# The gate product of a decoder block as seven products of halves, its last weight splits in vacated buffers, part of its gates added to x by transfers

## The chip, the cores and the metric

One Trainium2 chip, one of its cores. The metric is the device time of one execution in microseconds (us), the median of several runs. A profiled execution lists every instruction of the core's engines: TensorE (PE) with its weight loads (PEld), VectorE (DVE), ScalarE (ACT), GpSimd (POOL) and SyncE (SP), and the transfers that SP, ACT and POOL issue.

## What is computed

A decoder block on 512 rows of 1024 numbers, all in float32. Everything ahead of the last two products (a normalisation, one wide projection, a short convolution, four heads of a chunked recurrent attention, two output products) is cut here; it ends in `merged`. What matters:

```python
x = x + jnp.einsum('bsd,de->bse', merged, w_o[l])
gate = jax.nn.sigmoid(jnp.einsum('bsd,de->bse', rmsnorm(x, g_ple[l]), w_ple_gate[l]))
x = x + gate * jnp.einsum('bsp,pd->bsd', p[l], w_ple[l])
return rmsnorm(x, g_final)
```

Both weights are 1024 x 1024. The product with `w_ple` is made at the start of the kernel and waits in DRAM. `rmsnorm` is a row's factor times a column's: the column factor `g_ple` is multiplied in when x is turned, the row factor is the scale of the sigmoid.

## The kernel before

A float32 product is made of three TensorE passes on numbers cut in two: `hi` (rounded to float32r by ScalarE) and `lo` (the rest, a subtraction on VectorE). `mm3` (L215) issues hi*hi, hi*lo and lo*hi, each 128 rows x 128 x 512 columns. So every weight operand of 512 x 512 (1 MB, four blocks of 128 rows) is loaded by SP into one of four buffers (`load_raw`, L138), and split by halves of two blocks (`split_half`, L161): a ScalarE copy of 1024 elements a partition (L164), a VectorE subtraction of as many (L165). The split parts live in a ring of two operands (`wsplit`), so an operand can be split only when TensorE is done with the one two before it.

Most products are Strassen products in Winograd's form (`strassen`, L286): seven products of halves for eight, on sums of the operands. Sums on the weight side are made in the raw buffers, mostly by transfers that add (L171: POOL issues them after the split of a half, from the weight in DRAM); sums on the left side are made on VectorE. Sums of results are made by copying a bank of PSUM to SBUF (a snap, L333) and adding the next product's bank on VectorE (L337).

Work is written down in program order and each engine keeps that order. A generator (`tick`, `step`, L198 to L209) is stepped after every unit, the 12 matmuls of one row tile with one operand: first the newest tasks, then one half of a split from `pieces`, then the older tasks in `active`. A task's second piece is thus in the queues a unit later, and an instruction that waits holds back everything behind it on its engine.

The last two products are plain. `merged` is turned (the transposes `pth`, L1102) and cut into `mg`. The product with `w_o` has 16 units: two column halves, four row tiles, two operands. Each result tile goes through `add_residual` (L1163): a VectorE addition into `xr` (L1165), a ScalarE square with a row sum (L1167). `turn_to` (L1123) transposes x on TensorE (`ptk`, L1135) and cuts it into `h2` with `g_ple`. The gate's product has again 16 units. On its first column half `gated` (L1209) does a sigmoid from PSUM (ScalarE, L1213), a multiplication by the embedding `ple` (VectorE, L1214) and an addition into x (VectorE, L1215); then come the square (L1218) and x times `g_final` on POOL (L1224). `power` (L1242) takes a row's mean square to the power -1/2 on POOL (L1245), `final_scale` (L1247) refines it on VectorE, and `final` (L1254) makes the output tile and sends it out. On the last column half this follows tile by tile, the last tile in two column quarters of 256.

Of the kernel before, what the change touches and what calls it, by code (L numbers as in the profile page):

```python
# [14 lines left out]
P = 128  # L15
S = 512
# [20 lines left out]
def hybrid_block(ctx, tc, x, p, g_mix, w_in, conv_w, conv_b, w_a_out, b_gates, g_head,  # L37
# [117 lines left out]
    def split_tiles(i, h):  # L155

        parts = [wsplit.tile([P, HH, CW], F32R, name=f"w{u}{i}{h}", tag=f"w{u}{h}", align_bytes=256)
                 for u in ("hi", "lo")]
        splits.setdefault(i, []).append(parts)
        return raws[operands[i][0]][:, HH * h:HH * h + HH, :], *parts  # L160
# [19 lines left out]
    def queue_split():  # L180
        i = state["split"]
        if i < len(operands):
            state["split"] = i + 1
            pieces.extend((i, h) for h in range(2))
# [817 lines left out]
    m = mp.tile([P, NT, D], F32, name="m", tag="m")  # L1002
# [120 lines left out]
    def turn_to(dst, src, n, scale):  # L1123

        ks = range(n * HC, (n + 1) * HC)
        yield
        pts = {}
        for i in range(3):
            if i > 0:
                for k in ks[2 * i - 2:2 * i]:  # L1130
                    cut(dst[0][:, k, :], dst[1][:, k, :], pts[k], scale[:, k:k + 1])
            for k in ks[2 * i:2 * i + 2]:
                pts[k] = ps_x.tile([P, S], F32, name="ptk", tag="x")
                for t in range(NT):
                    pe.transpose(pts[k][:, t * P:(t + 1) * P], src[:, t, k * P:(k + 1) * P], ident)  # L1135
            yield


    ep_ctx, ep = open_pool("end")
    h2_ctx, h2p = open_pool("h2", side="right")  # L1140
    h2 = [h2p.tile([P, KT, S], F32R, name=f"h2_{i}", align_bytes=256) for i in range(2)]
    xr = ep.tile([P, NT, D], F32, name="xr")
    gfin = ep.tile([P, D], F32, name="gfin")
    ple = ep.tile([P, NT, D], F32, name="ple")
    ess = ep.tile([P, NT, 2], F32, name="ess")
    etot = ep.tile([P, NT], F32, name="etot")
    er = ep.tile([P, NT], F32, name="er")
    etmp = [ep.tile([P, NT], F32, name=f"etmp{i}") for i in range(3)]
    half = [slice(0, CW), slice(CW, D)]

    def load_end():
# [5 lines left out]
        for t in range(NT):  # L1157
            yield
            nc.gpsimd.dma_start(ple[:, t, :], ple_d[:, t, :])
        nc.gpsimd.dma_start(gfin, g_final.partition_broadcast(P))  # L1160

    def add_residual(n):
        def post(t, ps):  # L1163
# [4 lines left out]
            yield  # L1168
        return post

    ends = load_end()
    next(ends)
    active.append(ends)
    post = add_residual(0)
    pss = [None] * NT
    w = {}
    for c, ts in ((1, (0, 1)), (0, (0, 1)), (1, (2, 3)), (0, (2, 3))):
        if c not in w:  # L1180
            w[c] = next_operand(len(w) == 0)
        for t in ts:
            if c == 1:
                pss[t] = bank(t)
            for kt in range(HC):
                mm3(pss[t], [u[:, c * HC + kt, t * P:(t + 1) * P] for u in mg], [u[kt] for u in w[c]],
                    c == 1 and kt == 0, c == 0 and kt == HC - 1)
            if (c, t) == (1, 3):
                queue_split()
            step(post(t, pss[t]) if c == 0 else None)  # L1190
    active.append(turn_to(h2, xr, 0, gp))
    block_tm([(mg, 0), (mg, HC)], add_residual(1))
    active.append(turn_to(h2, xr, 1, gp))

    def norm_scale():
        yield
# [6 lines left out]
        dve.tensor_tensor(er, r, e, ALU.mult)  # L1203

    active.append(norm_scale())
    fss = ep.tile([P, NT, 4], F32, name="fss")
    xg = mp.tile([P, NT, D], F32, name="xg", tag="m")[:, :, half[0]]

    def gated(ps, t, c):  # L1209

        sl = xr[:, t, c]
        g = temp("e")[:, :c.stop - c.start]
        act.activation(g, ps, AF.Sigmoid, scale=er[:, t:t + 1])  # L1213
        dve.tensor_tensor(g, g, ple[:, t, c], ALU.mult)  # L1214
        dve.tensor_tensor(sl, sl, g, ALU.add)  # L1215

    def squares(t, c, i):
        act.activation(temp("c")[:, :c.stop - c.start], xr[:, t, c], AF.Square, accum_out=fss[:, t, i:i + 1])  # L1218

    def gate_embedding(t, ps):  # L1220
        gated(ps, t, half[0])
        yield
        squares(t, half[0], 0)
        pool.tensor_tensor(xg[:, t, :], xr[:, t, half[0]], gfin[:, half[0]], ALU.mult)  # L1224

    block_tm([(h2, 0), (h2, HC)], gate_embedding)

    base = ep.tile([P, NT], F32, name="base")
    wl = []

    def last_part(t, cs, a, b, ps):
        for c in cs:
            if c == len(wl):
                wl.append(next_operand())
            for kt in range(HC):
                mm3(ps[:, :b - a], [u[:, c * HC + kt, t * P:(t + 1) * P] for u in h2],
                    [u[kt][:, a:b] for u in wl[c]], c == 0 and kt == 0, c == 1 and kt == HC - 1)
            tick()
# [87 lines left out]
```

## Time and profile before

| what | value |
|---|---|
| median of 3 runs (lowest, highest) | 858.34 us (857.92, 858.58) |
| the profiled execution: its time, its span | 858.12 us, 856.3 us |
| mean granted TensorE clock | 0.997 |
| busy share: PE, DVE, ACT, POOL | 99%, 74%, 56%, 25% |
| first matmul of the product with w_o | 756.28 us |
| first matmul of the gate's product | 802.37 us |
| last matmul | 847.89 us |
| last output tile made | 852.5 us |

The span runs from the first to the last instruction of the core; the profiled execution's own time is 1.8 us more. Times inside the span are us from its start. A row of the timeline has a start, a duration, an engine, the line in the kernel, what is written and read, the shape, and in brackets how long the engine had been idle and for whom. The duration of a matmul is its passage through a pipeline; how far apart two starts lie is what it costs.

### The profile page before, as it was taken

What the parts mean: (1) busy time and instruction counts of PE and PEld (TensorE: products, weight loads), DVE (VectorE), ACT (ScalarE), POOL (GpSimd) and SP (SyncE); (2) the same over time, 40 slices, a digit from 0 to 9 for tenths busy, and PEclk for the clock granted to TensorE, in tenths of its full rate; (3) what the DMA queues carried; (4) which work ended last, traced back from release to release, by engine and by line L of the source; (5) the groups of instructions that cost most, each with busy time, mean ns of one, the idle gap of its engine ahead of it and who ended that gap; (6) DMA issues with size and microseconds to landing.
All of it is one profiled execution on the core that took longest, in us unless ns stands there. A gap on an engine that the chain in (4) does not pass through costs nothing.

```text
span 856.3 us, 12144 instructions
## 1 busy us (share of the span) xinstructions
PE 845.6 (99%) x4658; PEld 735.4 (86%) x4658; DVE 630.3 (74%) x813; ACT 483.4 (56%) x702; POOL 218.1 (25%) x221
## 2 busy tenths in 40 slices
PE   8999999999999999999999999999999999999996
PEld 6888888887889988888888999999998888888885
DVE  6786667976777676788677779897885788964465
ACT  6477665657755566665766654545543256634343
POOL 5103222203224332220223333342410222130031
PEclk9999999999999999999999999999999999999998
DMA  9749669779958998796998689999998487884002
GB/s 313 267 136 179 161 129 220 196 265 238 267 117 205 243 220 183 180 214 197 266 236 218 137 218 179 184 179 185 181 359 291 83 200 190 222 323 145 1 1 98
DMA packets 100139, 167.58 MB, mean 196 GB/s; under 512 B 5421, under 2 KB 45921, under 8 KB 98801
## 3 DMA queue, kind: packets, MB, share of 16 engines
q0 software_dynamic: 38672, 70.86, 43.0%
q1 hardware_dynamic: 58544, 90.97, 32.3%
q10 hardware_dynamic: 2864, 4.98, 1.6%
q8 instruction: 36, 0.59, 0.3%
q14 instruction: 23, 0.18, 0.1%
HBM read 150.01 MB, written 16.78 MB: 195 GB/s over the span
## 4 chain that ended last, share of the span: by engine, by line
PE 95%; DVE 2%; DMA 1%; issue 1%; ACT 1%; SPq 0%; POOL 0%; POOLq 0%; ACTq 0%
PE mm L217 29%; PE mm L218 29%; PE mm L219 29%; PE pv L217 1%; PE pv L219 1%; PE pv L218 1%; DMA xin<-in_x 1%; PE pty L799 1%; PE sc L219 1%; PE sc L218 1%; PE sc L217 1%; PE ptk L1135 0%; PE pth L1102 0%; PE pt L536 0%; DVE xin L531 0%
## 5 line engine op out<-in xcount | busy, mean ns | idle before, releaser
L165 DVE TENSOR_TENSOR wlo<-wraw,whi 128x1024 fp32r<-128x1024 f32 x238 | 298.3, 1256 | 118.6 <-ACT whi L164 117.8
L164 ACT ACTIVATE whi<-wraw 128x1024 fp32r<-128x1024 f32 x240 | 251.1, 1054 | 103.4 <-PE mm L219 44.5
L171 POOL DMA_DIRECT2D wraw<-in_w_in x112 | 136.7, 1418 | 316.9 <-DVE wlo L165 244.4
L333 ACT ACTIVATE s<-mm 128x512 f32<-128x512 f32 x84 | 50.2, 598 | 100.9 <-PE mm L219 99.6
L217 PE MATMUL mm<-whi,hs 128*128 128x512 f32 x256 | 99.9, 390 | 0.0
L218 PE MATMUL mm<-wlo,hs 128*128 128x512 f32 x256 | 99.8, 390 | 0.0
L219 PE MATMUL mm<-whi,hs 128*128 128x512 f32 x256 | 99.7, 389 | 0.0
L217 PE MATMUL mm<-hn_hi,whi 128*128 128x256 f32 (+1 forms) x304 | 93.4, 307 | 0.0
L219 PE MATMUL mm<-hn_hi,wlo 128*128 128x256 f32 (+1 forms) x304 | 93.0, 306 | 0.0
L218 PE MATMUL mm<-hn_lo,whi 128*128 128x256 f32 (+1 forms) x304 | 92.9, 306 | 0.0
L217 PE MATMUL mm<-hs,whi 128*128 128x256 f32 x320 | 90.9, 284 | 0.0
L218 PE MATMUL mm<-hs,whi 128*128 128x256 f32 x320 | 90.5, 283 | 0.0
L219 PE MATMUL mm<-hs,wlo 128*128 128x256 f32 x320 | 90.5, 283 | 0.0
L217 PE MATMUL mm<-whi,hn_hi 128*128 128x512 f32 x192 | 75.3, 392 | 0.0
L218 PE MATMUL mm<-wlo,hn_hi 128*128 128x512 f32 x192 | 75.0, 390 | 0.0
L219 PE MATMUL mm<-whi,hn_lo 128*128 128x512 f32 x192 | 74.7, 389 | 0.0
L218 PEld LDWEIGHTS mm<-hs,whi 128*128 128x128 f32 x320 | 61.4, 192 | 0.0
L217 PEld LDWEIGHTS mm<-hs,whi 128*128 128x128 f32 x320 | 61.4, 192 | 0.0
L219 PEld LDWEIGHTS mm<-hs,wlo 128*128 128x128 f32 x320 | 61.4, 192 | 0.0
L219 PEld LDWEIGHTS mm<-hn_hi,wlo 128*128 128x128 f32 x304 | 58.1, 191 | 2.8 <-POOL wlo L165 0.3
L218 PEld LDWEIGHTS mm<-hn_lo,whi 128*128 128x128 f32 x304 | 58.1, 191 | 2.4
L217 PEld LDWEIGHTS mm<-hn_hi,whi 128*128 128x128 f32 x304 | 58.1, 191 | 2.4
(306 smaller groups left out, 1673.7 us busy)
## 6 DMA issues: line engine op xcount, KB each, us to landing
wraw<-in_w_in SPq DMA_DIRECT2D x32, 1024.0 KB, 5.5
wraw<-in_w_in POOLq DMA_DIRECT2D x52, 512.0 KB, 7.7
wraw<-in_w_in SPq DMA_DIRECT2D x48, 512.0 KB, 5.4
wraw<-in_w_in POOLq DMA_DIRECT2D x60, 256.0 KB, 6.0
wraw<-in_w_b_out SPq DMA_DIRECT2D x7, 1024.0 KB, 6.4
wraw<-in_w_b_out POOLq DMA_DIRECT2D x12, 512.0 KB, 6.7
yt_d<-yc POOLq DMA_DIRECT2D x4, 1024.0 KB, 4.9
wraw<-in_w_a_out SPq DMA_DIRECT2D x4, 1024.0 KB, 5.5
```

Of the source, the lines that this page charges most:

```text
L164: act.activation(hi, t, AF.Copy)
L165: (e_lo or dve).tensor_tensor(lo, t, hi.bitcast(F32), ALU.subtract)
L171: nc.gpsimd.dma_start(raws[to][:, ks, cs], src[:, ks, :], accum_op=ALU.add)
L217: pe.matmul(ps, lhsT=a[0], rhs=b[0], start=first, stop=False, **kw)
L218: pe.matmul(ps, lhsT=a[0], rhs=b[1], start=False, stop=False, **kw)
L219: pe.matmul(ps, lhsT=a[1], rhs=b[0], start=False, stop=last, **kw)
L333: act.activation(to[i], src, AF.Copy, scale=scale)
L799: pe.transpose(pts[v][:, t * P:(t + 1) * P], y[:, t, v * P:(v + 1) * P], ident)
```

## The change

The gate's product becomes seven products. The four 512 x 512 quarters of x (called by row half and column half) are turned by `quarter` as soon as their rows are final, and `lefts` makes from them the seven left operands: three are quarters (`g_a11`, `g_a12`, `g_a22`), four are sums (`g_s1` to `g_s4`). Each is cut into hi and lo: 7168 elements a partition on ScalarE and as many on VectorE, where it was 4096 each; ScalarE's copies of the four quarters out of PSUM (4096) and VectorE's four sums (4096) come on top. The product with `w_o` goes through its row tiles by halves, in both column halves. The weight sums are made by transfers as elsewhere. TensorE's seven products run in the order g_a11, g_s1, g_a12, g_s2, g_s4, g_s3, g_a22, two units each, the last in column quarters of 256.

Three of the seven weight operands leave the ring: the first is split early into the place of the turned `m`, the sixth into the places of `g_a11` and `g_s1`, the seventh into the place of `mg`'s low part. `ple` now also takes the place of `m`, and so can be loaded only after the first product.

Results: row tiles 2 and 3 are finished by `g1` (columns 0 to 511) and `g3` (512 to 1023), the right half of tiles 0 and 1 by `g5`, their left half by `gated` at the end. In `g1` and `g3` the gate times the embedding is added to x by a transfer from SBUF to SBUF that adds (`embed` with `by_dma`), issued by POOL; the squares of these tiles are taken some ticks later. x times `g_final` on POOL is done for four tiles as before, but other ones (3 left and right, 0 right, 1 right), and four of the eight output tiles are made on ScalarE and sent from its own queue, where it was two.

```diff
-    for view in (w_o_v, w_pg_v):
-        for n in range(2):
-            block(view, [(n * CW, CW)], (HC, 0) if view is w_o_v and n == 0 else (0, HC))
+    for n in range(2):
+        block(w_o_v, [(n * CW, CW)], (0, HC) if n else (HC, 0))
+    early = len(operands)
+    g11, g21, g22, g12 = (chunk(w_pg_v, k, [(n * CW, CW)]) for k, n in ((0, 0), (HC, 0), (HC, 1), (0, 1)))
+    operands.extend([(g11, [(g11, g12, None)]), (g11, [(g11, g22, None)]), (g21, [(g12, g22, None)]),
+                     (g11, [(g11, g21, None)]), (g22, []), (g12, []), (g11, [])])
...
+    def cut_early():
+        for _ in range(5):
+            yield
+        u = mp.tile([P, 2, HC, CW], F32R, name="wearly", tag="m", align_bytes=128)
+        own[early] = [u[:, v] for v in range(2)]
+        pieces.extend((early, h) for h in range(2))
+    def load_ple():
+        u = mp.tile([P, NT, D], F32, name="ple", tag="m", align_bytes=128)
+        for t in (2, 3, 0, 1):
+            nc.gpsimd.dma_start(u[:, t, :], ple_d[:, t, :])
...
+    def lefts(h, n):
+        v1, v2 = by_two(b1), by_two(b2)
+        if (h, n) == (0, 0):
+            yield from quarter(h, n, v1)
+        elif (h, n) == (1, 0):
+            yield from quarter(h, n, v2)
+            yield
+            cut(*g_a11, b2)
+            s3 = two_temps("gs3")
+            for i in range(2):
+                dve.tensor_tensor(s3[i], v2[i], v1[i], ALU.subtract)
+            yield
+            cut_by_two(g_s3, s3)
+        elif (h, n) == (0, 1):
+            f22 = two_temps("gf22")
+            yield from quarter(h, n, f22)
+            for i in range(2):
+                dve.tensor_tensor(v1[i], f22[i], v1[i], ALU.subtract)
+            act.activation(g_s1[0], b1, AF.Copy)
+            cut_by_two(g_a22, f22)
+            yield
+            dve.tensor_tensor(g_s1[1], b1, g_s1[0].bitcast(F32), ALU.subtract)
+            dve.tensor_tensor(b2, b1, b2, ALU.add)
+            yield
+            act.activation(g_s2[0], b2, AF.Copy, scale=-1.0)
+            dve.scalar_tensor_tensor(g_s2[1], b2, -1.0, g_s2[0].bitcast(F32), ALU.mult, ALU.subtract)
+        else:
...
+            yield from quarter(h, n, f12)
+            cut_by_two(g_a12, f12)
+            yield
+            for i in range(2):
+                dve.tensor_tensor(v1[i], v2[i], f12[i], ALU.subtract)
+            yield
+            cut(*g_s4, b1)
...
+    def embed(c, t, cols, by_dma=False):
+        sl = xr[:, t, cols]
+        dve.tensor_tensor(c, c, ple[t][:, cols], ALU.mult)
+        if by_dma:
+            nc.gpsimd.dma_start(sl, c, accum_op=ALU.add)
+        else:
+            dve.tensor_tensor(sl, sl, c, ALU.add)
...
+    def gate(c, ps, t, scale):
+        dve.tensor_tensor(c, c, ps, ALU.add)
+        act.activation(c, c, AF.Sigmoid, scale=scale[:, t:t + 1])
+    def g3(i):
+        t = 2 + i
+        c = sn[i]
+        gate(c, cc[i], t, ner)
+        yield
+        embed(c, t, half[1], True)
+        yield
+        yield
+        yield
+        squares(t, half[1], 1)
+        power(t, 1)
+        if t == 3:
+            weigh(t, 1)
+    def g5(i):
+        gate(sv[i], acc[i], i, ner)
+        yield
+        embed(sv[i], i, half[1])
+        squares(i, half[1], 0)
+        weigh(i, 1)
+        add_base(i, 0)
...
+    last_part(0, 0)
+    tick()
+    last_part(1, 0)
+    tick()
+    gated(0, 0)
+    last_part(0, 1)
     drain()
+    gated(1, 0)
+    squares(0, q[0], 1)
+    add_base(0, 1)
     final_scale(2)
+    final(2, 0)
+    last_part(1, 1)
+    gated(0, 1)
+    squares(1, q[0], 1)
+    add_base(1, 1)
+    gated(1, 1)
+    squares(0, q[1], 2)
+    power(0, 2)
     final(2, 1)
+    squares(1, q[1], 2)
+    power(1, 2)
     final_scale(3)
     final(3, 0, True)
+    final(3, 1, True)
+    final_scale(0)
+    final(0, 1, True)
+    final(0, 0)
+    final_scale(1)
+    final(1, 1, True)
+    final(1, 0)
```

Three places show how the instructions stand. On VectorE, the middle of the gate's product before (operand halves `wlo`, then `gated` of the first column half):

```order
L165 TENSOR_TENSOR wlo_7555<-wraw_7264,whi_7554 128x1024
L1214 TENSOR_TENSOR e<-e,ple 128x512
L1215 TENSOR_TENSOR xr<-xr,e 128x512
L165 TENSOR_TENSOR wlo_7575<-wraw_7264,whi_7574 128x1024
L1214 TENSOR_TENSOR e<-e,ple 128x512
L1215 TENSOR_TENSOR xr<-xr,e 128x512
```

And now, from the row factor of the norm (`etmp`, which POOL's power feeds) to the second half of the fourth operand; `fx` and `glb` belong to the left operand g_s4, `wlo_7614` and `wlo_7636` are the halves of the fourth weight operand, L1348 is the addition in `gate`:

```order
L242 TENSOR_TENSOR etmp_7119<-etmp_7117,etmp_7118 128x4
L243 TENSOR_TENSOR etmp_7119<-etmp_7119,etmp_7118 128x4
L244 TENSOR_SCALAR etmp_7119<-etmp_7119 128x4
L1260 TENSOR_TENSOR er<-etmp_7118,etmp_7119 128x4
L1261 TENSOR_SCALAR ner<-er 128x4
L1236 TENSOR_TENSOR fx<-fx,gf_7533 128x512
L1236 TENSOR_TENSOR fx<-fx,gf_7534 128x512
L173 TENSOR_TENSOR wlo_7614<-wraw_7091,whi_7613 128x1024
L235 TENSOR_TENSOR glb<-fx,glb 128x1024
L1348 TENSOR_TENSOR gs<-gs,mmb 128x512
L173 TENSOR_TENSOR wlo_7636<-wraw_7091,whi_7635 128x1024
```

The left operand's sums and cuts, and the results' additions, now stand between the halves of the weights.

On POOL, from the loads of x to the first output's powers, before:

```order
L1154 DMA xr<-in_x 128x512 x8
L1159 DMA ple<-ple_d 128x1024 x4
L1160 DMA gfin<-in_g_final 128x1024
L1200 TENSOR_TENSOR etmp_7120<-etmp_7119,mhalf 128x4
L1224 TENSOR_TENSOR xg<-xr,gfin 128x512 x4
L1245 TENSOR_TENSOR etmp_7120<-etmp_7119,mhalf 128x1 x4
```

The same place now (L179 are the adding transfers of the weights, L1297 those of the gates):

```order
L1149 DMA xr<-in_x 128x512 x8
L1152 DMA gfin<-in_g_final 128x1024
L179 DMA wraw_7091<-in_w_ple_gate 128x2x512 x4
L179 DMA wraw_7342<-in_w_ple_gate 128x2x512 x2
L1165 DMA ple<-ple_d 128x1024 x4
L1257 TENSOR_TENSOR etmp_7118<-etmp_7117,mhalf 128x4
L179 DMA wraw_7091<-in_w_ple_gate 128x2x512 x2
L1297 DMA xr<-gs 128x512 x2
L1334 TENSOR_TENSOR xg<-xr,gfin 128x512
L1297 DMA xr<-gs 128x512 x2
```

The power for the norm's row factor (L1257) now stands behind six adding transfers and the four loads of `ple`.

On ScalarE, the end before (`e` are the gates, `c` the squares, `y` the outputs):

```order
L1213 ACTIVATE e<-mm,er 128x256
L1218 ACTIVATE c,fss<-xr 128x256
L1213 ACTIVATE e<-mml,er 128x256
L1260 ACTIVATE y<-xg,fs 128x512
L1263 DMA out<-y 128x512
L1218 ACTIVATE c,fss<-xr 128x256
L1260 ACTIVATE y<-xg,fs 128x512
L1263 DMA out<-y 128x512
```

And now (`gs` the gates of `g3` and `g5`, `eq` those of the last quarters, `fsq` the squares):

```order
L1349 ACTIVATE gs<-gs,ner 128x512 x2
L1302 ACTIVATE fsq,fss<-xr 128x512 x3
L1425 ACTIVATE eq<-mm,er 128x256
L1302 ACTIVATE fsq,fss<-xr 128x512
L1425 ACTIVATE eq<-mm,er 128x256
L1302 ACTIVATE fsq,fss<-xr 128x256
L1425 ACTIVATE eq<-mm,er 128x256
L1302 ACTIVATE fsq,fss<-xr 128x256
L1425 ACTIVATE eq<-mm,er 128x256
L1302 ACTIVATE fsq,fss<-xr 128x256 x2
L1324 ACTIVATE y<-xg,fs 128x512
L1327 DMA out<-y 128x512
```

Four squares of whole tiles stand among the gates of the last quarters; three more pairs of output and issue follow the last rows shown, where before there were two pairs in all.

More of the change, by code (lines that the diff above doesn't have):

```diff
@@ new lines, in load_ple, with left_pair @@
+    def load_ple():
+        u = mp.tile([P, NT, D], F32, name="ple", tag="m", align_bytes=128)
+        for t in (2, 3, 0, 1):
+            nc.gpsimd.dma_start(u[:, t, :], ple_d[:, t, :])
+        ple.extend(u[:, t, :] for t in range(NT))
+    def left_pair(pool_, tag=None):
+        u = pool_.tile([P, 2, HC, H2], F32R, name="gl", tag=tag, align_bytes=256)
+        return [u[:, v] for v in range(2)]
+    g_a11, g_s3, g_s1, g_a22, g_s2 = (left_pair(glp, f"gl{i}") for i in range(5))
+    g_a12, g_s4 = [], []
@@ L1168, in post @@
             yield
-        return post
[L1173 to L1193, printed above, removed]
+            if t % 2:
+                yield from lefts(t // 2, n)
+        return post
     def norm_scale():
+        yield
         yield
@@ L1205, in hybrid_block @@
     active.append(norm_scale())
     fss = ep.tile([P, NT, 4], F32, name="fss")
[L1207 to L1218, printed above, removed]
```

209 lines of the change are left out of this document (131 added, 78 removed).

## The prediction

> **What bounds the kernel now.** I read the page first (span, TensorE's row), then TensorE's waits, then each engine's timeline from 735 us on.
>
> ```profile
> span 856.3 us, 12144 instructions
> PE 845.6 (99%) x4658; PEld 735.4 (86%) x4658; DVE 630.3 (74%) x813; ACT 483.4 (56%) x702; POOL 218.1 (25%) x221
> PE mm L477 <- DVE hn_lo L472: 1.5, 1, 1.5
> ...
> PE mmp L591 <- ACT whi L569: 0.2, 1, 0.2
> ```
>
> TensorE is busy all the time, and its few waits lie in the start-up. So each matmul removed is worth its distance to the next, as long as ScalarE and VectorE deliver in time. Where the last two products stand, from the chain of waits, and their pitch and end, from TensorE's timeline:
>
> ```profile
> 756.28 0.23 PE mm L217
> 764.46 0.88 PE pth L1102 x8
> 784.41 0.87 PE ptk L1135 x8
> ...
> 802.37 0.39 PE L217 MATMUL mm<-whi,h 128*128 128x512 f32 x1
> 805.09 0.39 PE L217 MATMUL mm<-whi,h 128*128 128x512 f32 x1
> 842.26 0.28 PE L217 MATMUL mm<-whi,h 128*128 128x256 f32 x1
> 847.89 0.28 PE L219 MATMUL mml<-whi,h 128*128 128x256 f32 x1
> ```
>
> Twelve matmuls take 805.09 - 802.37 = 2.72 us: 0.227 each, 2.72 a unit. The last matmul ends at 848.17. What follows it, from the timelines:
>
> ```profile
> 848.21 0.47 ACT L1213 ACTIVATE e<-mml,er 128x256 f32<-128x256 f32 x1 [0.44 <-PE mml L219]
> 848.71 0.42 DVE L1214 TENSOR_TENSOR e<-e,ple 128x256 f32<-128x256 f32 x1 [0.25 <-ACT e L1213]
> 849.17 0.42 DVE L1215 TENSOR_TENSOR xr<-xr,e 128x256 f32<-128x256 f32 x1
> 849.51 0.21 DVE L1298 TENSOR_SCALAR base<-fss,base 128x1 f32<-128x1 f32 x1
> 849.71 0.42 ACT L1218 ACTIVATE c<-xr 128x256 f32<-128x256 f32 x1 [0.42 <-DVE xr L1215]
> 851.80 0.72 ACT L1260 ACTIVATE y<-xg,fs 128x512 f32<-128x512 f32 x1 [1.58 <-POOL etmp L1245]
> 852.55 0.36 ACTq L1263 DMA_DIRECT2D out<-y  x1
> ```
>
> The last output is made 4.35 us after the last matmul (852.52), and 3.8 us later the span ends. The execution's own time, 858.12, is 1.8 above the span and 0.2 below the median of 858.34; I sum against 858.12.
>
> **What is removed.** The gate's product had 16 units; seven products of two are 14. That is 24 matmuls less, at 0.227 each 5.44 us. The transposes (four groups of eight) and the 48 matmuls of 256 columns stay. Without a wait TensorE would end at 848.17 - 5.44 = 842.73.
>
> **What is added** is work on ScalarE and VectorE, in a fixed order and much of it in alternation. The rows that price it:
>
> ```profile
> 803.98 1.99 ACT L164 ACTIVATE whi<-wraw 128x1024 fp32r<-128x1024 f32 x2
> 805.06 2.36 DVE L165 TENSOR_TENSOR wlo<-wraw,whi 128x1024 fp32r<-128x1024 f32 x2 [1.80 <-ACT whi L164]
> 817.98 0.69 ACT L1213 ACTIVATE e<-mm,er 128x512 f32<-128x512 f32 x1 [3.02 <-PE mm L219]
> 818.56 1.05 ACT L164 ACTIVATE whi<-wraw 128x1024 fp32r<-128x1024 f32 x1
> 819.43 0.69 DVE L1215 TENSOR_TENSOR xr<-xr,e 128x512 f32<-128x512 f32 x1
> 820.04 1.22 DVE L165 TENSOR_TENSOR wlo<-wraw,whi 128x1024 fp32r<-128x1024 f32 x1
> 821.28 0.62 ACT L1218 ACTIVATE c<-xr 128x512 f32<-128x512 f32 x1
> 821.80 0.19 ACT L1218 ACTIVATION_READ_ACCUMULATOR c<-xr 128x1 f32 x1
> 728.16 1.20 POOL L171 DMA_DIRECT2D wraw<-in_w_b_out  x1 [3.44 <-DVE wlo L165]
> 757.49 1.06 POOL L1159 DMA_DIRECT2D ple<-ple_d  x2 [0.20 <-issue]
> 807.78 1.03 POOL L1200 TENSOR_TENSOR etmp<-etmp,mhalf 128x4 f32<-128x4 f32 x1 [46.18 <-DVE etmp L1199]
> ```
>
> In a queue a 1024-wide ScalarE copy takes 0.94 (1.99 - 1.05), a VectorE operation of 1024 columns 1.14 (2.36 - 1.22), one of 512 columns 0.61 (820.04 - 819.43). A 512-wide ScalarE operation takes 0.5 to 0.6 (818.56 - 817.98), a square 0.61 with its sum. A hand-over to another engine adds 0.13: the tail of the operation and 0.04. POOL takes 1.2 for an adding transfer's issue, 0.53 for a load of ple, 1.03 for the norm's power.
>
> I follow the last thing that each step waits for. Its start is the w_o product's eleventh unit. With the order of row halves and the transposes it ends at 756.28 + 11 x 2.72 + 0.88 + 2 x 0.87 = 788.82; from there on no wait in this chain is one for TensorE.
>
> Leg one, from that bank to x's last tile (row L1243 in the new kernel): on VectorE ten of 512 (four of them x, the others the sums and cuts of g_s3, g_s1, g_a22), 6.1, and five of 1024 (g_a11, both halves of the second weight operand, g_s1, the sum for g_s2), 5.7; on ScalarE three of 1024, 2.8, two squares and three of 512, 2.8; seven hand-overs, 0.9. Sum 18.3: 807.2. TensorE wants the tile for its last transposes at 788.82 + 7 x 2.72 + 0.87 = 808.7, so this is still in time.
>
> Leg two, to the norm's power: square 0.6, ScalarE's copies for the third operand's halves and g_s2, 3 x 0.94, a snapshot 0.5, VectorE's low half 1.14; then POOL, which has the issue of that half's adding transfer (1.2), the four loads of ple (2.1) and only then the power (1.03); hand-overs 0.4. Sum 9.8: 817.0. Queued behind that wait on VectorE are all rows that follow L242: the factor itself, g_s4, the fourth weight operand, the first gates.
>
> Leg three: five tiny operations 1.0, two of 512 for g_s4's sum 1.2, its cut 0.94 and 1.14, the first gate's addition 0.61, sigmoid 0.55, and only behind it on ScalarE the fourth operand's second half, 0.94 and 1.22; hand-overs 0.5. Sum 8.1: the high part at 823.9, the low part at 825.2. TensorE starts this product at 756.28 + 22 x 2.72 + 0.88 + 4 x 0.87 = 820.5 and wants the second half 1.36 later, at 821.8: it waits 2.1 for the high part and 1.0 for the low part, 3.1 in sum. If the power were free, 2 of these would go and the wait for the low part would stay; so 1 to 3.
>
> Leg four, to the second gate of tile 3: three gate additions 1.9, two sigmoids 1.1, two high halves 1.9, six low halves 6.8, two multiplications by ple 1.2, a tiny one 0.15, four hand-overs 0.5: 13.6. To this comes what POOL's x times g_final does to VectorE:
>
> ```profile
> 820.36 2.05 POOL L1224 TENSOR_TENSOR xg<-xr,gfin 128x512 f32<-128x512 f32 x1 [11.54 <-DVE xr L1215]
> 821.42 1.53 DVE L1214 TENSOR_TENSOR e<-e,ple 128x512 f32<-128x512 f32 x1 [0.17 <-ACT e L1213]
> ```
>
> VectorE's multiplication, 0.69 alone, took 1.53 and ended 0.54 after POOL (822.41): it was held. POOL's first such product meets the last low half here, 1.1. Leg four ends at 839.9. The Trainium skill (SBUF — State Buffer, section "SBUF: two separate sides") calls the pair of ports that VectorE and GpSimd share an exclusive lock, held for the whole instruction, when VectorE reads two SBUF inputs; by that rule, the trace agrees, with the 1.53 beside 0.69.
>
> Leg five, the end. Sigmoid, square, tiny base and product with ple, 2.2: 842.1. Then the adding transfer of tile 2's second half. Before has no such transfer inside SBUF; the nearest are the adding transfers of the weights (first row: least, median and most from issue to landing); the outputs and ple are plain ones:
>
> ```profile
> DMA to landing us min/median/max: 4.4/6.4/14.0
> ple<-ple_d POOLq DMA_DIRECT2D x4, 512.0 KB, 10.5
> out<-y SPq DMA_DIRECT2D x6, 256.0 KB, 2.1
> ```
>
> At this place little else moves, so I take 4.5: 846.6. Bounds: 2.1, the plain output's, which saves 0.8 (the square then waits for the one ahead of it), and 8, which costs 3.5 more. The Trainium skill (DMA: Bandwidth & Descriptors, section "Anatomy of one DMA — SWDGE (gpsimd) path") gives about 2.0 us and the bytes at 436 GB/s, 2.6 for 256 KB, by which the sum would be some 0.7 lower; the row's 4.4 is above it even at its best. Behind the landing: square and base 0.9, tile 1's multiplication and addition 1.5, its square 0.6, then on ScalarE a quarter's sigmoid, the square of tile 3 and another sigmoid, 1.6: 851.2. Then VectorE alone: three pairs of 256 columns (0.46 + 0.35 each) 2.4, four tiny 0.8, two factors of three operations 1.2, two outputs 1.5: 857.1. Then ScalarE: four outputs at 0.72 and three issues at 0.36 between them, 4.0: 861.1. From there 3.75 to the end: 864.9, and 1.8: **866.7 us**, 8.6 above 858.12. In the sum: 5.4 removed, but the end moves from 4.35 behind the last matmul to about 14 behind where it would have ended, because the chain of ScalarE and VectorE, not TensorE, ends last; of TensorE's own waits (3.1, and 2.7 more before the last product, whose bank the gate of tile 0 still reads) none adds to that.
>
> What costs nothing: by the same tally each transfer that sums weights has at least 10 us from its issue to the split that reads it, above the row's median of 6.4; ple is issued at 813.8, lands by the row's 10.5 at 824.3, and is first read in leg four at 828.6. If that cover goes, each late us moves the chain by one.
>
> A measurement of this kernel can tell about 0.2%, 1.7 us.
>
> **The rivals.** First, faster: the chain keeps ahead of TensorE, so its last matmul ends at 842.7. Then the end is: sigmoid and two quarter operations 1.4, tiny ones and an output on VectorE 1.7, ScalarE's 4.0, 3.75 and 1.8: 855.4, 2.7 faster. For it speaks that VectorE was nearly full elsewhere and TensorE waited for nothing:
>
> ```profile
> 700.00:740.00 40.00, 40.00 (x183) 33.20 (x182) 35.83 (x37) 23.35 (x27) 9.03 (x9) 1.00 0.81 187
> ```
>
> (35.83 of 40 us is VectorE.) Against it: here a unit of the third product asks for addition, sigmoid, high half and low half one behind the other, 0.69 + 0.58 + 1.05 + 1.22 = 3.5 in 2.72. It decides whether the fourth operand's low half is done by 822. Chance 0.10.
>
> Second, no change: the feed keeps up, but the end is serial all the same. From g5's second gate at 836.8, two tiles' multiplications, additions and squares take 4.6, and the way from tile 1's square to the last output is 12.1 as in leg five: 853.5, with 5.55 behind it 859.1. Chance 0.12. It decides whether the transfer's landing is off the path.
>
> Third, slower still: the adding transfer takes 8 or more, as the weights' worst did, or POOL's products hold VectorE three more times: 870 and above. Chance 0.08. That the change doesn't do what it says, eight products left or the sums made otherwise, is excluded by the order of the instructions: TensorE has 24 fewer.
>
> **How the numbers follow.** The forecast has 0.70: 861 to 870, from the free power (-2), the transfer's bounds (-0.8, +3.5), and 5% on a chain of 72 us, of which I take off 3 at the low end. Below it lie 859.1 (0.12) and 855.4 (0.10). The range from 858.0 to 870.5 leaves out the faster case and part of the third, 0.16 in all. Faster by over 0.2% is 0.10; within it, 0.12; slower 0.78.
>
> **What would show it.** Right: TensorE idle for 2 to 3 us in the fourth product, ended by a high and a low part of a weight half; POOL's four-wide power near 816; VectorE's first tiny operation behind it; no matmul in the last 12 us of the span; the last outputs one after the other on ScalarE. Wrong: TensorE without waits and a last matmul near 842.7; the power done before 813; the transfer's landing before the square is reached.

## The result and the profile after

The changed kernel takes 864.13 us (median of 4 runs, 863.01 to 864.67), the kernel before 858.41 (4 runs, 857.92 to 858.58; the 858.34 above is of three of them): a ratio of 1.0066, 95% interval 1.0049 to 1.0083, slower by 5.7 us. The forecast was 866.7, with a range from 858.0 to 870.5. The profiled execution of the changed kernel took 864.67 us; its lines are compared with those of before's profiled execution at 858.12.

The page of the changed kernel, its span and busy shares, and TensorE's waits (what waited, for whom; total, times and longest in us):

```profile
span 862.9 us, 12184 instructions
PE 844.0 (98%) x4634; PEld 734.1 (85%) x4634; DVE 643.0 (75%) x835; ACT 501.7 (58%) x737; POOL 230.8 (27%) x233
PE mm L227 <- ACT eq L1425: 3.6, 1, 3.6
PE mm L227 <- DVE gs L1348: 2.1, 1, 2.1
PE mm L228 <- DVE wlo L173: 0.7, 1, 0.7
```

TensorE has 24 matmuls fewer, and three waits that before has not. The 0.7 lies in the fourth product, the 2.1 ahead of the last product, the 3.6 in its middle. The last was not in the forecast. TensorE's timeline there, and two windows of each engine's busy time from 846 on (the granted clock is the third number from the end, 1.00 is full):

```profile
847.10 0.58 PE L227 MATMUL mm<-wlast,gl 128*128 128x256 f32 x1 [3.56 <-ACT eq L1425]
852.17 0.41 PE L229 MATMUL mm<-wlast,gl 128*128 128x256 f32 x1
...
846.00:849.00 3.00, 1.90 (x9) 1.90 (x10) 2.01 (x8) 2.53 (x8) 2.05 (x3) 0.50 0.00 0
849.00:853.00 4.00, 3.59 (x17) 3.29 (x16) 3.10 (x8) 1.24 (x5) 1.14 (x1) 0.53 0.17 66
```

The third quarter piece writes one half of a bank of whose other half the first sigmoid still has to read, and it comes behind that sigmoid. Behind the wait the clock stands at 0.50, and the last 24 matmuls take 5.07 us from first to last, 0.22 each. The last matmul starts at 852.17; before's started at 847.89. The last output is made at 859.73, before's at 852.52. So 4.3 of the 7.2 us lie ahead of TensorE's end and 2.9 behind it.

The legs of the forecast, from the timelines of the changed kernel; each row is the step that ends a leg or stands on the way:

```profile
798.91 4.91 POOL L179 DMA_DIRECT2D wraw<-in_w_ple_gate  x4 [15.16 <-DVE wlo L173]
806.67 0.68 DVE L1243 TENSOR_TENSOR xr<-xr,mm 128x512 f32<-128x512 f32 x1
809.70 2.18 POOL L1165 DMA_DIRECT2D ple<-ple_d  x4 [5.88 <-issue]
812.61 0.15 DVE L1255 TENSOR_TENSOR etot<-ess 128x4 f32<-128x4 f32 x1
813.06 1.03 POOL L1257 TENSOR_TENSOR etmp<-etmp,mhalf 128x4 f32<-128x4 f32 x1 [1.18 <-DVE etmp L1256]
815.14 0.15 DVE L242 TENSOR_TENSOR etmp<-etmp,etmp 128x4 f32<-128x4 f32 x1
821.98 1.23 DVE L173 TENSOR_TENSOR wlo<-wraw,whi 128x1024 fp32r<-128x1024 f32 x1 [1.74 <-ACT whi L172]
834.86 2.02 DVE L173 TENSOR_TENSOR wlast<-wraw,wlast 128x1024 fp32r<-128x1024 f32 x1 [1.74 <-ACT wlast L172]
836.86 0.67 DVE L1348 TENSOR_TENSOR gs<-gs,mm 128x512 f32<-128x512 f32 x1
839.00 0.68 DVE L1295 TENSOR_TENSOR gs<-gs,ple 128x512 f32<-128x512 f32 x1
840.23 0.87 POOL L1297 DMA_DIRECT2D xr<-gs  x1 [4.43 <-DVE gs L1295]
843.58 0.63 ACT L1302 ACTIVATE fsq<-xr 128x512 f32<-128x512 f32 x1
847.56 0.46 ACT L1425 ACTIVATE eq<-mm,er 128x256 f32<-128x256 f32 x1
848.98 1.18 DVE L1315 SCALAR_TENSOR_TENSOR etmp<-etmp,etmp 128x1 f32<-128x1 f32 x1
853.13 0.42 DVE L1295 TENSOR_TENSOR eq<-eq,ple 128x256 f32<-128x256 f32 x1 [0.89 <-ACT eq L1425]
855.27 0.16 DVE L1317 TENSOR_TENSOR fs<-etmp,etmp 128x1 f32<-128x1 f32 x1
859.01 0.72 ACT L1324 ACTIVATE y<-xg,fs 128x512 f32<-128x512 f32 x1 [0.47 <-ACT y L1324]
```

### The profile page after: what moved, and what is told of

Read it like the earlier page. It is cut to its first block, busy times and chain, and to the rows that moved or that the text cites. A ratio compares the mean times of both kernels' runs of the same rounds, so it can differ in the third digit from the quotient of the medians.

```text
span 862.9 us, 12184 instructions
## 1 busy us (share of the span) xinstructions
PE 844.0 (98%) x4634; PEld 734.1 (85%) x4634; DVE 643.0 (75%) x835; ACT 501.7 (58%) x737; POOL 230.8 (27%) x233
## 4 chain that ended last, share of the span: by engine, by line
PE 90%; DVE 4%; ACT 3%; issue 1%; DMA 1%; SPq 0%; ACTq 0%; POOL 0%; DVEq 0%
PE mm L227 27%; PE mm L228 27%; PE mm L229 27%; PE pv L227 1%; PE pv L229 1%; PE pv L228 1%; DMA wraw<-in_w_ple 1%; PE pty L809 1%; PE sc L229 1%; PE sc L228 1%; PE sc L227 1%; ACT whi L172 1%; DVE wlo L173 0%; DVE gs L1295 0%; DVE gs L1348 0%
## 5 line engine op out<-in xcount | busy, mean ns | idle before, releaser
L179 POOL DMA_DIRECT2D wraw<-in_w_in x112 | 136.8, 1421 | 317.4 <-DVE wlo L173 236.6
```

Source lines behind the costliest of these rows:

```text
L179: nc.gpsimd.dma_start(raws[to][:, ks, cs], src[:, ks, :], accum_op=ALU.add)
```

## The experiments

The theory of the forecast (chain, C): ScalarE and VectorE take their work in a fixed order, and how long that order is sets the end. Two rivals: TensorE's waits and its low clock set it (TensorE, W), or the landing of the adding transfers does (transfer, T). All ratios below are to the kernel before on the same chip (its median was 858.41 us in the first row, 858.05 to 858.11 in the others), with 95% intervals. The rows come from several chips, so a few tenths of a microsecond between two rows say little.

| run | us, median | ratio | last matmul starts | last output made |
|---|---|---|---|---|
| changed kernel | 864.13 | 1.0066 [1.0049, 1.0083] | 852.17 | 859.73 |
| quarter pieces first | 863.87 | 1.0064 [1.0052, 1.0077] | 847.74 | 859.28 |
| filler matmuls | 863.30 | 1.0061 [1.0048, 1.0074] | 849.56 | 858.36 |
| additions on VectorE | 867.05 | 1.0103 [1.0088, 1.0119] | 854.74 | 862.16 |
| first sigmoid later, wrong tile | 863.59 | 1.0064 [1.0051, 1.0077] | 851.44 | 858.99 |
| first sigmoid later | 864.13 | 1.0065 [1.0052, 1.0078] | 851.79 | 859.35 |
| all through the ring | 870.90 | 1.0151 [1.0137, 1.0165] | 858.31 | 865.87 |
| before, 24 matmuls fewer | 853.78 | 0.9948 [0.9935, 0.9960] | 843.06 | 847.70 |
| one order | 856.94 | 0.9985 [0.9976, 0.9994] | 842.98 | 851.96 |
| its tail alone | 863.05 | 1.0060 [1.0047, 1.0073] | 845.31 | 856.92 |
| its front alone | 860.45 | 1.0028 [1.0017, 1.0040] | 848.08 | 855.50 |
| front, pieces first | 859.83 | 1.0021 [1.0012, 1.0031] | 842.33 | 854.84 |
| one order, tuned | 857.42 | 0.9991 [0.9983, 1.0000] | 842.31 | 851.47 |

The last two columns are of each kernel's profiled execution.

**Are TensorE's last wait and its clock on the path?** All four quarter pieces go ahead of the first sigmoid:

```diff
-    gated(0, 0)
     last_part(0, 1)
+    last_part(1, 1)
+    gated(0, 0)
...
     final(2, 0)
-    last_part(1, 1)
```

> All four quarter pieces of the last product are issued ahead of the first sigmoid of the end, so that the third piece no longer waits 3.6 us for that sigmoid and TensorE's clock stays up. Theory C (the chain of ScalarE and VectorE ends last, TensorE's waits count only where the halved clock delays the last sigmoid): the last gate starts earlier but VectorE is not free then; the time falls by 1.4 us, to about 862.7. Theory W (TensorE's waits count in full): it falls by 3.6 of wait and 2.7 of slow clock, to about 858. Theory T (the adding transfers of the gates hold the squares): no change, 864.

```profile
PE mm L227 <- DVE gs L1348: 2.1, 1, 2.1
...
847.74 0.28 PE L229 MATMUL mm<-wlast,gl 128*128 128x256 f32 x1
853.61 0.42 ACT L1302 ACTIVATE fsq<-xr 128x256 f32<-128x256 f32 x1 [0.34 <-DVE xr L1299]
```

The 3.6 us wait is gone and the last matmul starts 4.4 us earlier, but the last output comes only 0.45 earlier. VectorE's wait of 0.89 for the last sigmoid is gone; one of 0.40 for the second sigmoid has come (at 848.62). The last square waits for VectorE, not for TensorE. So TensorE's theory falls: what TensorE loses in this wait is nearly all covered by the chain. But the 1.4 us that the chain theory expected didn't come either, and the time is the one that the transfer theory gave; the third experiment decides between these two.

**The clock alone.** Thirteen matmuls into a spare bank keep TensorE busy during the wait:

```diff
+    filler = ps_x.tile([P, S], F32, name="filler", tag="x")
+    for _ in range(13):
+        pe.matmul(filler, lhsT=g_a22[0][:, 0, :P], rhs=w[0][0], start=True, stop=True)
     gated(0, 0)
```

> Thirteen matmuls on a spare bank, whose result nobody reads, fill TensorE's wait ahead of the third quarter piece; the wait itself stays. C: the granted clock stays 1.0 in the last two pieces, they take 2.9 us and not 5.5, and the time falls by 1.4 us as when the wait is taken away, to about 862.7. W: only the slow clock goes, 2.7 us, 861.4. If the slow clock has another cause than the idle time, it stays and the time with it, 864.

```profile
842.97 3.14 PE L1434 MATMUL filler<-wlast,gl 128*128 128x512 f32 x13
...
846.00:848.00 2.00, 1.40 (x12) 1.30 (x12) 1.43 (x5) 1.97 (x8) 1.06 (x2) 1.00 0.00 0
```

The clock stays at 1.00 and the last matmul comes 2.6 us earlier. The median falls by 0.8 us, less than the chain theory (1.4) and TensorE's (2.7) expected, and its interval overlaps that of the changed kernel: of the halved clock about this much at most was on the path.

**The transfers.** The gates' additions go back to VectorE, so that no transfer inside SBUF is left:

```diff
-        if by_dma:
+        if False:
```

> The four gates that transfers add to x are added by VectorE instead. C: four more operations of 0.61 us in VectorE's queue and no landing to wait for: 2.4 us more, about 866.5. T: the squares no longer wait for a landing of 3 to 4 us, the time falls by 2 us or more, 862. W: no change but what the last product waits longer, 865.

```profile
PE mm L227 <- DVE gs L1348: 4.0, 1, 4.0
PE mm L227 <- ACT eq L1425: 2.7, 1, 2.7
```

Four operations more on VectorE cost 2.9 us, though four landings are gone. The chain theory expected 2.4 more, the transfer theory 2 less: in this order it is the chain, not the transfers. The wait ahead of the last product grows to 4.0, because its gate stands behind the added work.

**The fourth product's wait.** The sigmoid of the third product's gate goes behind the next split half on ScalarE. A first version multiplied the embedding into the wrong snapshot; the second multiplies it into the gate's own:

```diff
-        gate(sn[i], bb[i], t, er)
-        yield
-        embed(sn[i], t, half[0], True)
+        c = sn[i]
+        dve.tensor_tensor(c, c, bb[i], ALU.add)
+        yield
+        act.activation(c, c, AF.Sigmoid, scale=er[:, t:t + 1])
+        yield
+        embed(c, t, half[0], True)
```

> The sigmoids of tiles 2 and 3, first column half, are issued one unit after their additions, so that ScalarE's next weight half no longer stands behind them. C: the wait in the fourth product (0.7) goes, VectorE's idle pieces of 1.7 us in the third to fifth product go, the second g5 gate starts about 2 us earlier, and the end comes 2 us earlier: 862.2. W: 0.7 us, 863.4. T: no change, 864.

> The run before this one meant to move the sigmoid of the third product's gate behind the next split half on ScalarE, but multiplied the embedding into the wrong snapshot. Here the gate's own tile is kept, so the output is the reference's; nothing else differs from the changed kernel. Chain theory (ScalarE and VectorE take their work in a fixed order, and each end of the changed kernel hangs on how late a split half or a gate comes in that order): the fourth product's wait of 0.7 us goes, the sixth product starts earlier, and the end moves from 864.1 to 862.8 us (861.5 to 863.5). TensorE theory (the waits that TensorE still has, and its lower clock behind them, set the end): the 3.6 us wait for the bank of the first sigmoid stays, only the 0.7 goes, 863.4. Transfer theory (the adding transfers set the end): they are issued a unit later, 864 to 866.

The waits of the second version:

```profile
PE mm L227 <- ACT eq L1428: 3.8, 1, 3.8
PE mm L227 <- DVE gs L1348: 1.5, 1, 1.5
```

VectorE's timeline of the second version, from the first gate of the sixth product to its second:

```profile
837.23 0.68 DVE L1348 TENSOR_TENSOR gs<-gs,mm 128x512 f32<-128x512 f32 x1
839.32 0.15 DVE L1311 TENSOR_SCALAR base<-fss 128x1 f32<-128x1 f32 x1 [1.40 <-ACT fsq L1302]
839.39 1.18 DVE L1295 TENSOR_TENSOR gs<-gs,ple 128x512 f32<-128x512 f32 x1
840.49 0.68 DVE L1348 TENSOR_TENSOR gs<-gs,mm 128x512 f32<-128x512 f32 x1
```

The 0.7 is gone, and the time is the same: 864.13, where the chain expected 862.8 and TensorE 863.4. The first of these gates comes 2.4 us earlier than in the changed kernel (839.60), the second only 0.3 (840.80). Between them VectorE stands 1.40 behind a small operation that waits for a square, and its product with ple, 0.68 elsewhere, takes 1.18 beside POOL's first weighing. So the order gives back at the next place what it gained at the last. The time is the one that the transfer theory gave, but no step of this stretch waits for a landing, and the third experiment had spoken against that theory.

**What the extra places are worth.** All seven operands go through the ring:

```diff
-    active.append(cut_early())
...
-        w = next_operand(left is not g_s1)
+        w = next_operand()
...
-            own[i] = [glp.tile([P, HC, CW], F32R, name="wlate", tag=f"gl{v}", align_bytes=256) for v in (0, 2)]
...
-        if left is g_s2:
-            own[early + 6] = last
```

> The changed kernel without its extra places: all seven operands of the gate's product are split into the two-deep ring, so no operand is split early into the place of m or late into the places of used left operands. Chain theory: each split then waits until TensorE has left the ring's slot, the second operand's split waits for its adding transfer behind that, and TensorE waits about 4 us at the second product and again at the last: 868 to 872 us. Rival (the places move only work that is hidden anyway): 863.6 to 864.6, no change.

```profile
PE mm L227 <- ACT whi L172: 2.8, 2, 2.1
PE mm L228 <- DVE wlo L173: 2.6, 4, 0.9
```

The places are worth 6.8 us, as the chain theory said, though the waits are spread over six places of up to 2.1 and not two of 4. This part of the change does what it says.

**What 24 matmuls are worth.** The kernel before without 24 of its gate's matmuls (the first row half of the weights with row tiles 0 and 1, first column half), nothing added:

```diff
+            if c == 1 or t > 1:
                 for kt in range(HC):
                     mm3(pss[t], ...)
```

> The kernel before with 24 of the gate's matmuls left out (the products of the first row half of the weights with row tiles 0 and 1 in the first column half), so its output is not the reference's; as many matmuls as the change removes, with no other work added. If TensorE alone bounds the kernel before at this place: 24 times 0.227 is 5.4 us, so 852.7 us (852 to 854). Rival (other engines bound the end of the kernel before too, so matmuls removed from the gate's product are given back): 855 to 858.

```profile
843.06 0.28 PE L219 MATMUL mml<-whi,h 128*128 128x256 f32 x1
846.98 0.72 ACT L1270 ACTIVATE y<-xg,fs 128x512 f32<-128x512 f32 x1 [1.58 <-POOL etmp L1255]
```

The time falls by 4.3 us of the 5.4: the removed matmuls were on the path of the kernel before, and the last output still comes 4.6 us behind the last matmul's start. So what the change removes is worth 4.3 us when nothing is added.

**The order, all of it.** From the third product on, the operations are issued by a list instead of the generators. They are the same but for the last product, which is made whole: 24 matmuls of 512 columns in place of 48 of 256, and six operations fewer on VectorE and on ScalarE each. In the list hi and lo are split halves, g1a and g1s gate additions and sigmoids, e..m products with ple, y outputs, p4i1k0 a group of three matmuls:

```diff
-            step(post(i))
...
+    for n in TABLE.split():
+        one(n)
+    # hi31 p2i1k1 hi51 p2i1k2 g1a0 lo31 p2i1k3 hi41 p3i0k0 g1a1 hi40
+    # ...
+    # eq00 p21 q11 pw21 e00a pw31 f2a e00b wg11 f2b b11 fs2 f3a eq10 y21
...
-        (nc.scalar if on_act else nc.sync).dma_start(out[0, t * P:(t + 1) * P, half[n]], y)
+            nc.sync.dma_start(out[0, t * P:(t + 1) * P, half[h]], y)
```

> The changed kernel's own instructions from the third product on, in another order on ScalarE, VectorE and GpSimd: split halves ahead of gates where both are ready, gates of the third and fifth product a little later, the last product whole (24 matmuls of 512 columns in place of 48 of 256) ahead of its first sigmoid, the outputs of row tiles 2 and 3 as soon as their scale is there, all outputs issued by SyncE. Chain theory (the order of the added work costs, not its amount): TensorE waits nowhere in the seven products, its last matmul ends near 842, the last output is made near 848.7, the whole 854.5 us (853.5 to 857), below the kernel before. Rival by amount (ScalarE and VectorE have more to do behind TensorE's end than before, in whatever order): 859 to 863. Transfer theory (landing times of the adding transfers set the end): 860 to 862.

TensorE's only wait in the seven products, a square that waits for an adding transfer, TensorE's last matmul, the last outputs on both engines, and the issues of outputs on SyncE's queue:

```profile
PE mm L228 <- DVE wlo L173: 0.3, 1, 0.3
...
840.76 0.63 ACT L1385 ACTIVATE fsq<-xr 128x512 f32<-128x512 f32 x1 [0.46 <-DMA xr<-gs]
842.98 0.39 PE L229 MATMUL mm<-wlast,gl 128*128 128x512 f32 x1
851.18 0.75 DVE L1495 SCALAR_TENSOR_TENSOR y<-xr,fs,gfin 128x512 f32<-128x512 f32 x1
851.24 0.72 ACT L1493 ACTIVATE y<-xg,fs 128x512 f32<-128x512 f32 x1 [0.51 <-DVE fs L1475]
846.71 6.07 SPq L1496 DMA_DIRECT2D out<-y  x8
```

The time is 7.2 us below the changed kernel and 1.2 below the kernel before (the interval just leaves out 1). It comes by the order, by the whole last product (1.0 us less busy time on VectorE, 0.8 on ScalarE) and by who issues the outputs, together. The rivals by amount (859 to 863) and by transfers (860 to 862) fall. The upper part of the range, 857, is met, not 854.5: the last output is made at 851.96, 3.3 later than the 848.7 worked out. In that tail the small power takes POOL 0.9, where it took 0.54 in the kernel before, and VectorE's 0.2 us operations beside POOL's products up to 1.0. In this order a landing does stand on the path: the square at 840.76 waits 0.46 us for an adding transfer, and the chain that ended last runs through it.

**Which part of the order.** The tail alone, and the front alone:

```diff
-    last_part(0, 0)
-    tick()
-    last_part(1, 0)
+    whole(0)
+    tick()
+    whole(1)
...
-    final(1, 0)
+    result(1, 0)
```

> The changed kernel as it is through the sixth product, and only what follows in another order: the last product whole and ahead of its first sigmoid, the outputs of row tiles 2 and 3 between the gates of tiles 0 and 1, every output issued by SyncE. It tells which part of the order of e6 gives the time back. Chain theory in two parts (each part of the order costs what lies on the path there): the sixth product still comes as late as in the changed kernel, its gates at 839.6 and 840.8, the first sigmoid of the last product at 846.6; from there 2.4 us for two embeddings, 2.6 for four outputs on VectorE and some 3 of small operations lead to a last output near 855.2, so 861 us (860 to 862.3). Rival one (the tail's order is the whole loss): 857 to 858. Rival two (all is set by when the sixth product's gates come): 864.

> The other part of e6 alone: its order of split halves and gates from the third to the sixth product, and behind these the tail in the changed kernel's order (quarter pieces, the first sigmoid between them, outputs of tile 3 and then of tiles 0 and 1 at the end, ScalarE issuing its own). Chain theory in two parts: the gates of the sixth product come 2 us earlier and the tail keeps its length, so 862 us (861 to 863). Rival one (the tail's order is the whole loss): 864. Rival two (all is set by when the sixth product's gates come): 857 to 859.

The last matmul and output of the tail alone, then the remaining wait, the last matmul and the last output of the front alone:

```profile
845.31 0.39 PE L229 MATMUL mm<-wlast,gl 128*128 128x512 f32 x1
856.17 0.72 ACT L1432 ACTIVATE y<-xg,fs 128x512 f32<-128x512 f32 x1 [0.58 <-DVE fs L1317]
```

```profile
PE mm L227 <- ACT eq L1540: 3.5, 1, 3.5
848.08 0.28 PE L229 MATMUL mm<-wlast,gl 128*128 128x256 f32 x1
854.78 0.72 ACT L1324 ACTIVATE y<-xg,fs 128x512 f32<-128x512 f32 x1 [0.47 <-ACT y L1324]
```

The front gives 3.7 us, the tail 1.1, both together 7.2. The front has every operation of the changed kernel, so its 3.7 are order alone; the tail has the whole last product and SyncE's issues as well, and its 1.1 is not clear of noise (the intervals overlap). Both times lie outside their expected ranges: the front was underrated (2 expected), the tail overrated (3). Of the tail's 2.8 us up to the last output (859.73 to 856.92), 1.1 goes again behind it: its span ends 4.3 behind the last output, the changed kernel's 3.2 (862.9 - 859.73). All eight outputs are in SyncE's queue there; that this is the reason was not tried. Why the two parts together give 2.4 more than their sum stays open.

**Front, and pieces first.** The same edit as in the first experiment, on the front alone:

> The run with e6's front (split halves and gates in e6's order) and the changed kernel's tail, now with the four quarter pieces ahead of the first sigmoid as in the first experiment, so that TensorE waits for no sigmoid and is done before its clock falls. It asks whether TensorE's last wait, 3.5 us in that run, and the lower clock behind it come onto the path once the gates come earlier. Chain theory (VectorE, without a gap from 843.3 to 853.1 in that run, and ScalarE's outputs behind it set the end whatever TensorE does): 859.5 to 860.5 us, as that run. TensorE theory (with an earlier front the wait and the clock are what is left): 3.5 and some 1.2 us of halved clock go from the last sigmoid, 856 to 857.5.

```profile
842.33 0.28 PE L229 MATMUL mm<-wlast,gl 128*128 128x256 f32 x1
845.56 0.46 ACT L1540 ACTIVATE eq<-mm,er 128x256 f32<-128x256 f32 x1
```

The last matmul comes 5.7 us earlier than with the front alone, the last sigmoid 2.8 (848.40 to 845.56), the end 0.6 (the intervals overlap). With the gates early, too, TensorE's wait costs the end next to nothing.

**A tuned order:**

> e6 with its order worked out again from the durations that its own trace shows (a power of one column at 0.9 us on GpSimd in place of 0.5, small operations of VectorE held while GpSimd weighs a tile): the embedding of row tile 1 ahead of the second output of tile 2, and the weighing of tile 1 behind the powers. Chain theory: VectorE's last output ends 1.4 us earlier than in e6, 855.5 us (854.7 to 856.5), below the kernel before by 0.3%. Rival (the tail is at its bound by amount): 856.9, as e6.

Not faster than the first list (857.42 against 856.94). Its profiled execution makes the last output 0.5 earlier, its median is 0.5 later; the 1.4 didn't come. What is left of the tail is 9 us in both lists: all of tiles 0 and 1's first column half has its sigmoids, embeddings, squares, scales and outputs behind the seventh product, where before has only a quarter of one tile and 4.6 us.

## Why the prediction was right, and where it was not

The forecast said: 5.4 us of TensorE's work go, the end moves further back behind the last matmul, and ScalarE and VectorE's chain ends last. That held, and the experiments bear it out: moving TensorE's end by 4.4 and 5.7 us moves the time by 0.3 and 0.6 (pieces first, twice), four more operations on VectorE move it by 2.9, and another order moves it by 3.7 by itself, by 7.2 together with the whole last product and the outputs on SyncE.

Step by step, the forecast's time for the end of each leg and the measured one:

| step | forecast | measured | what it was |
|---|---|---|---|
| leg one, x's last tile | 807.2 | 807.35 | as worked out |
| leg two, norm's power done | 817.0 | 814.1 | POOL was free |
| leg three, low part | 825.2 | 823.2 | 9.1 us long, not 8.1 |
| leg four, second gate of tile 3 | 839.9 | 837.5 | 14.3 long, not 14.7 |
| product with ple | 842.1 | 839.7 | 2.2, as worked out |
| transfer of tile 2 | 846.6 | by 843.6 | 3.9 or less, not 4.5 |
| sigmoid of the second piece | 851.2 | 848.0 | 4.4, not 4.6 |
| factor of tile 3 | 857.1 | 855.4 | 7.4, not 5.9 |
| last output | 861.1 | 859.7 | 4.3, not 4.0 |
| end of span | 864.9 | 862.9 | 3.2, not 3.75 |

The step that failed is leg two: "then POOL, which has the issue of that half's adding transfer". The third operand's transfers don't stand there. Row 798.91 shows four issues running without a gap, done by 803.8, so that at 809.7 POOL has only ple's loads, and the power follows at 813.06, as soon as its input is made. That input was late for another reason: VectorE makes its first part at 812.61, behind three operations of 1024 columns that stand ahead of it from 809.09 on. At 815.14 VectorE's first small operation follows the operation ahead of it without a wait for POOL. Two of the power's 2.9 us came through to the low part, since VectorE itself was not free before 815.1. The forecast had this as a bound ("if the power were free, 2 of these would go"), and the fourth product waits 0.71 where it had 3.1. In the run with the first sigmoid later this wait is gone and the time the same.

POOL's lock on VectorE, reckoned at 1.1 in leg four, is there with 0.8: 2.02 for a low half that takes 1.22 alone. The transfer's 4.5 was too much: issued at 840.23, it landed 3.3 us later, and the square at 843.58 follows the one ahead of it on ScalarE without a wait, 3.9 behind the product with ple. So the landing was hidden, as at the lower bound; the forecast had named that as a sign of being wrong.

Not seen: the third piece's wait of 3.56 us for the first sigmoid, by the bank's other half, and the clock behind it. Together with one small operation that POOL held for 1.18, they make leg five's VectorE part 1.5 longer: the last sigmoid made VectorE wait 0.9. So the forecast's "no matmul in the last 12 us" failed as well: the last one ends at 852.6, 10.3 ahead of the end. The forecast said that none of TensorE's waits adds to the sum; by the first two experiments the 3.56 us and the clock behind them add about 0.8 at most. The wait ahead of the last product, 2.7 in the forecast and 2.14 here, was not taken away by itself.

The sum is 2.0 too high: 2 for the power, 0.6 for the transfer, 0.55 behind the last output and small parts of the other legs too much, 1.8 in the last steps too little. The direction didn't hang on any of them; but misses of nearly 4 us one way and 2 the other stand behind an error of 2, so that the closeness of the number is in part luck. And the end does not move to "about 14" us behind where TensorE would have ended: by the forecast's own sum the last output lies 861.1 - 842.7 = 18.4 behind it, measured 17.0.

What the forecast also left out: how much of the chain is its order. It priced the order as written, and rightly so; but nearly the same work in a better order ends 1.2 us below the kernel before, so the seven products by themselves need not lose. Of the 7.2 us between the two, 4.3 go by order alone (the front with pieces first, 859.83); how the rest divides between the tail's order, the whole last product and SyncE's issues is not shown. In the best order that was run, 4.4 of the 5.4 us saved go into a tail of 9.0 in place of 4.6 us behind the last matmul's start.

## What to carry to other kernels

When matmuls are removed by adding sums and splits on the other engines, write those engines' queues out in order to the last output; a wait of TensorE's at the end, here 3.6 us with a halved clock behind it, can cost next to nothing (here about 0.8 us at most). Then ask what must come behind the last matmul: a form in which the last product completes two tiles at once leaves more behind it than one that completes a quarter of one, and that eats most of the saving. Where an operation is issued (an adding transfer's issue ahead of a power on POOL) is to be read from the order, not assumed from who uses it.

## What the runs showed of the hardware

The granted clock fell to 0.50 in TensorE's wait of 3.56 us (the changed kernel) and stayed at 1.00 when fillers bridged that wait. The mean of 0.96 in the window from 845 to 846 puts the fall at 845.9, 2.4 us after TensorE's last matmul before the wait had ended (843.54). In the first experiment the clock fell also behind the wait of 2.13 us ahead of the last product: the mean of 0.54 puts that fall at 841.1, 2.7 us after the wait began and 0.5 us after TensorE had resumed. In the changed kernel the same wait of 2.14 left it at 1.00. The changed kernel's window, then the first experiment's matmul and window:

```profile
845.00:846.00 1.00, 0.00 (x0) 0.00 (x0) 0.83 (x2) 0.04 (x1) 0.64 (x2) 0.96 0.03 2
...
840.54 0.36 PE L227 MATMUL mm<-wlast,gl 128*128 128x256 f32 x1 [2.13 <-DVE gs L1348]
841.00:842.00 1.00, 1.00 (x8) 1.00 (x7) 1.00 (x2) 0.53 (x2) 0.21 (x1) 0.54 0.27 47
```

The Trainium skill (TensorE: Matmul & The Clock Gate, section "Part 1: The HAM clock gate") puts the fall behind an idle window of about 3.4 us that runs freely. These two falls don't agree with that: they came 2.4 and 2.7 us after the waits began, sooner than a whole window of that length, and the second when TensorE was busy again.

A matmul into one half of a bank and a sigmoid that reads the other half came one behind the other here (3.56 us). The Trainium skill (PSUM — Partial Sum Buffer, section "PSUM bank collisions raise a hardware error") asks for guards by bank and quadrant, not by address; the order in the trace agrees. Issued ahead of the first reader of its other half, as in the first experiment, work on the second half of a bank had no such wait.

The changed kernel's four adding transfers of 256 KB inside SBUF took 3.3 to 3.9 us from issue to landing (median 3.6); POOL spent 0.85 to 0.89 us on each issue.
